# Gain of the heads on the transposed outputs, a GLA state of 128 columns, one query product, and a later first gate

## The chip, the cores and the metric

The kernel runs on one core of one Trainium2 chip. TensorE (PE) does the matrix products, with its weight loads shown apart (PEld); VectorE (DVE), ScalarE (ACT) and GpSimd (POOL) do the elementwise work; SyncE (SP) issues nearly all transfers. Each of these engines works through its own list of instructions in order. The metric is the time of one execution on the device, in microseconds, as the median of the runs.

## What is computed

A decoder layer over 2048 tokens of width 1024, in fp32, in two sub-layers, with a final norm.

```python
mod = (silu(c) @ w_ada + b_ada)                     # six rows of 1024
sh1, sc1, g1, sh2, sc2, g2 = split(mod, 6)
h = rms_norm(x) * (1 + sc1) + sh1
x = x + g1 * token_mixer(h, ...)
h = rms_norm(x) * (1 + sc2) + sh2
x = x + g2 * conv_ffn(h, ...)
return rms_norm(x) * final_gain

# in token_mixer, for 4 retention, 8 HGRN2 and 4 GLA heads of 64 values
proj = h @ w_in
o_n = attn_n @ v_n + (q_n * decay_n) @ S            # per chunk n
S   = decay * S + k_n^T @ v_n                       # GLA keys: 32 per head, others 64
o   = rms_norm(o) * silu(gate)                      # per head
return (concat(o_retention, o_hgrn2, o_gla) * head_gain) @ w_out
```

The conv_ffn has width 2816, a causal convolution of width 3 and a gated product.

## The kernel before

**Tiling.** The token mixer runs over four blocks b of 512 tokens, the conv FFN after it over two halves of 1024 tokens. Activations are kept transposed, features on the 128 partitions and tokens along the row. Every product of fp32 operands is split in a rounded high part and the rest, so it is three matmuls (`split3`, lines 246 to 248 in the function of that name): high by high, high by low, low by high. The normed input of a block is eight tiles `ha` (high and low), made from the input tiles `xn` (lines 352, 356 and 359).

**Units.** In each block the order is h0, g0, h1, h2, h3, r0, r1: four HGRN2 units of two heads, one GLA unit of four heads, two retention units of two heads. A unit projects its queries, keys, values and gates from the block's normed input, weight piece by weight piece, and hands the recurrent part to a chain of steps. After r1 follows the normed input of block b+1 and then the first half of the output projection (`out_half`); the second half (`out_finish`) comes after h0 of the next block. `out_finish` also adds the gated result to x and prepares the second norm, whose write-out for block 0 is put off until the conditioning it needs is there.

**Weight pieces.** `piece` loads 1024 columns of weight (512 KB) into one of the two `wraw` slots, ACT rounds it to the high part and DVE takes the difference as the low part. The low part is kept in memory on the first use, so later blocks fetch it. For the output projection the piece is multiplied by the heads' gain in that step, in four parts of 256 columns with a gain each (lines 236 and 239), and both parts are kept.

**Conditioning.** The 48 columns of mod are made by `ada`: a transfer of 512 KB into a `wraw` slot (line 190) and one reduction on DVE (line 197). The first 16 are made at the start. The rest wait in the list `later`, and each call of `piece` (and each quarter of the GLA value projection, `tf512`) first takes one from it. Columns 16 to 23 are the first gate (G1), which the first output projection needs; 24 to 39 are shift and scale of the second norm; 40 to 47 the second gate.

**The recurrent part.** A state S holds, for two heads, 64 columns of values each: keys on partitions, values along the row. For HGRN2 and retention S is block diagonal, 128 columns wide. For GLA the state of a pair has 64 columns; the two heads lie on different partitions. `attn_out` makes the outputs of a pair per chunk of 128 tokens. For HGRN2 and retention that is one matmul of all queries (`qn`, both heads stacked) by the state, and one of the scores by the values for each head. For GLA it is, for each head, one of the scores by the values (line 578) and one of that head's queries by the state (line 581). Queries for the scores lie in `qbd` tiles, [128, 2, 512], a plane for each head with zeros elsewhere; DVE multiplies query by decay separately for each head's rows into its plane (lines 719, 720 and 771), and ACT gathers `qn` from the planes (line 655). `transposed` turns the normed and gated outputs into `oT`, high part on ACT (line 561) and low part on DVE (line 562), for the output projection.

**Order of the work.** PE's order is that of the program. A small clock (`Clock`) adds up how long its matmuls take (`adv`), and steps of the chains are put between the projections when their due time is reached (`at`, `chain`). `rstd` makes the reciprocal root of a row norm in two steps on PE: the sum (`ssn`, line 325) and, a gap of 4.5 us by that clock later, its broadcast (`bcn`, line 335). The orders of DVE, ACT and SP are made by a scheduler from the program, with priorities given by `high_priority`.

**Constants.** `vec` has 245 columns: conditioning biases, gains, and, from column 61, the convolution's weights and biases and the final gain.

## Time and profile before

| | |
|---|---|
| median of 3 runs | 2576.79 us (2573.41 to 2576.92) |
| profiled execution | 2578.24 us |
| its span, first to last instruction | 2576.2 us |
| mean granted clock of TensorE | 0.993 |
| HBM read, written | 397.72 MB, 133.69 MB |

The stages follow from the windows of the profile: the start until about 60 us, block 0 until about 328 us, the later blocks and the last output projection until about 1300 us, then the conv FFN.

How to read it: the page's first part gives busy time of each engine, its share of the span and the count of instructions. A row of the groups or of the timeline has the line of the kernel, the engine, the operation, output and inputs by the program's names, and partitions by elements; in brackets stands how long the engine was idle before it and what ended that. The table of waits sums such idle time by who was waited for. The granted clock is that of TensorE, as a share of full speed. A timeline row of a fp32 matmul of 128 or 64 columns counts two passes ("x2") for one matmul of the program.

### The profile page before, as it was taken

How to read it: one execution, taken by the hardware profiler on the slowest of the kernel's cores; microseconds unless marked ns; L12 is line 12 of the kernel's file. 1: busy time of each engine (PE TensorE's matmuls, PEld its weight loads, DVE VectorE, ACT ScalarE, POOL GpSimd, SP SyncE). 2: the span in 40 equal slices, each digit the busy share in tenths (PEclk: the TensorE clock that was granted, in tenths of full speed). 3: DMA queues.
4: the chain of work that ended last, by engine and by line, in shares of the span. 5: the costliest groups of instructions: out<-in, count | busy, mean ns of one | idle time of the engine just before them, and what ended most of it. 6: DMA issues, size and time to landing. Idle time of an engine off the chain costs nothing.

```text
span 2576.2 us, 37281 instructions
## 1 busy us (share of the span) xinstructions
PE 2500.8 (97%) x13206; PEld 2137.1 (83%) x13206; DVE 1990.0 (77%) x3648; ACT 1116.4 (43%) x1898; POOL 168.7 (7%) x302
## 2 busy tenths in 40 slices
PE   5999999999999999999899999999989999999998
PEld 4798877998889888998788888888878888888887
DVE  8778986868778786887688888886677778778666
ACT  3433434433343234433254545555444455455442
POOL 1000010000000000000200000000001101000000
PEclk9999999999999999999999999999999999999999
DMA  8543656765687856877754444477675444447653
GB/s 302 200 155 132 214 215 227 272 217 178 212 303 271 293 176 211 316 265 258 264 186 164 163 135 163 156 256 244 220 231 169 145 154 146 145 143 245 225 191 128
DMA packets 229194, 533.89 MB, mean 207 GB/s; under 512 B 25072, under 2 KB 28176, under 8 KB 229008
## 3 DMA queue, kind: packets, MB, share of 16 engines
q1 hardware_dynamic: 224528, 516.83, 58.7%
q0 software_dynamic: 4480, 14.68, 1.6%
q8 instruction: 104, 1.70, 0.3%
q14 instruction: 82, 0.67, 0.1%
HBM read 397.72 MB, written 133.69 MB: 206 GB/s over the span
## 4 chain that ended last, share of the span: by engine, by line
PE 80%; issue 9%; DVE 6%; DMA 3%; ACT 2%; POOL 0%; SPq 0%; DVEq 0%; ACTq 0%; POOLq 0%
PE X L246 6%; PE X L248 6%; PE X L247 6%; PE lvh L622 3%; PE Z L246 3%; PE Z L248 3%; PE Z L247 3%; PE psqkvgr L248 2%; PE psqkvgr L246 2%; PE psqkvgr L247 2%; PE psvgh L246 2%; PE psvgh L247 2%; PE psvgh L248 2%; PE y L246 2%; PE y L248 2%
## 5 line engine op out<-in xcount | busy, mean ns | idle before, releaser
L246 PE MATMUL X<-B,A 128*128 128x512 f32 x572 | 223.7, 391 | 1.4 <-ACT u L1261 1.4
L247 PE MATMUL X<-B,A 128*128 128x512 f32 x572 | 222.9, 390 | 0.0
L248 PE MATMUL X<-B,A 128*128 128x512 f32 x572 | 222.8, 390 | 0.0
L988 DVE TENSOR_TENSOR dA<-rd,dA 128x512 fp32r<-128x512 f32 x154 | 106.0, 689 | 88.3 <-ACT dA L987 88.1
L987 ACT CAST dA<-rd 128x512 fp32r<-128x512 f32 x154 | 95.6, 621 | 139.8 <-PE dY L248 45.9
L988 DVE TENSOR_TENSOR A<-s,A 128x512 fp32r<-128x512 f32 x176 | 120.7, 686 | 40.5 <-ACT A L987 40.0
L987 ACT CAST A<-s 128x512 fp32r<-128x512 f32 x176 | 108.6, 617 | 72.4 <-PE Z L248 46.8
L246 PE MATMUL psvgh<-hvgh,ha 128*128 128x256 f32 x480 | 139.9, 291 | 0.0
L246 PE MATMUL dX<-dB,dA 128*128 128x512 f32 x352 | 136.9, 389 | 0.0
L247 PE MATMUL dX<-dB,dA 128*128 128x512 f32 x352 | 136.9, 389 | 0.0
L248 PE MATMUL dX<-dB,dA 128*128 128x512 f32 x352 | 136.9, 389 | 0.0
L248 PE MATMUL psvgh<-hvgh,ha 128*128 128x256 f32 x480 | 135.6, 283 | 0.0
L247 PE MATMUL psvgh<-lvgh,ha 128*128 128x256 f32 x480 | 135.6, 283 | 0.0
L246 PEld LDWEIGHTS X<-B,A 128*128 128x128 f32 x572 | 107.7, 188 | 24.4 <-ACT u L1261 2.2
L247 PEld LDWEIGHTS X<-B,A 128*128 128x128 f32 x572 | 107.7, 188 | 22.4
L248 PEld LDWEIGHTS X<-B,A 128*128 128x128 f32 x572 | 107.6, 188 | 22.4
L622 PEld LDWEIGHTS lvh<-qbh,kh 128*128 128x128 f32 x896 | 115.1, 190 | 7.8 <-issue 1.6
L246 PE MATMUL Z<-B,A 128*128 128x512 f32 x308 | 120.4, 391 | 0.0
L622 PE MATMUL lvh<-qbh,kh 128*128 128x128 f32 x896 | 120.1, 276 | 0.3 <-DVE kh L632 0.3
L247 PE MATMUL Z<-B,A 128*128 128x512 f32 x308 | 120.3, 391 | 0.0
L248 PE MATMUL Z<-B,A 128*128 128x512 f32 x308 | 120.3, 391 | 0.0
L988 DVE TENSOR_TENSOR dB<-rb,dB 128x512 fp32r<-128x512 f32 x154 | 105.4, 686 | 9.6 <-ACT dB L987 9.5
(460 smaller groups left out, 7145.9 us busy)
## 6 DMA issues: line engine op xcount, KB each, us to landing
gs<-yv SPq DMA_DIRECT2D x154, 256.0 KB, 3.0
rb<-gs SPq DMA_DIRECT2D x154, 256.0 KB, 3.9
r<-wup SPq DMA_DIRECT2D x141, 256.0 KB, 3.3
s<-sumsu SPq DMA_DIRECT2D x132, 256.0 KB, 3.0
wada<-wada SPq DMA_DIRECT2D x48, 512.0 KB, 5.0
rd<-sumsd SPq DMA_DIRECT2D x88, 256.0 KB, 3.8
rd<-wdown SPq DMA_DIRECT2D x66, 256.0 KB, 3.7
x<-xT SPq DMA_DIRECT2D x64, 256.0 KB, 5.0
```

What stands on the lines that cost most here:

```text
L246: T.matmul(ps, lhs[0], rhs[0], start=first, stop=False, skip_group_check=more)
L247: T.matmul(ps, lhs[0], rhs[1], start=False, stop=False, skip_group_check=more)
L248: T.matmul(ps, lhs[1], rhs[0], start=False, stop=last, skip_group_check=more)
L622: T.matmul(ps[:, c * P:(c + 1) * P].rearrange("p (h n s) -> p h n s", h=2, s=s), kq[:, c * P:(c + 1) * P], rhs, start=True, stop=True)
L987: S.copy(hi, src)
L988: V.tensor_tensor(lo, src, hi, op=ALU.subtract)
```

## The change

It has six parts.

1. The heads' gain is no longer multiplied into the pieces of the output weight, but into the transposed outputs, where the gain is one value for each partition: ACT's copy becomes a copy with a scale, DVE's difference a scaled difference. `both` keeps high and low part of the piece as before.
2. The GLA states have 128 columns, block diagonal like the others, and are cleared at the start. `attn_out` has one form for all: one matmul of all queries by the state, then one of scores by values for each head.
3. Query times decay is one DVE operation over all partitions, in place, and ACT copies the rows into the planes of `qbd`. The stacked queries are plane 0, after the rows of the second head have been copied into it. The tile `qn` of these units is gone.
4. Columns 16 to 23 of the conditioning are taken from `later` by the pieces from h2 on (with three places left empty), and no longer from g0 on; columns 24 to 39 after h0 of block 1, and no longer from its start. The put-off write-out of block 0 and the sums of the FFN's weights in block 1 come one unit later.
5. The gap between sum and broadcast is 8.0 us for the first norm of the next block and for the second norm of all blocks but the last.
6. `vec` has the first 117 columns; the others (`vec2`, 184 columns from column 61) are loaded after the mixer's buffers are released, before the last `out_finish`; the convolution and the final gain read it (not shown below). The mask has 320 columns instead of 448.

```diff
@@ -137,10 +137,10 @@
 
-    vec = pc.tile([P, NV], F32, tag="vec", name="vec")
-    nc.sync.dma_start(vec[:], vecs)
+    vec = pc.tile([P, 117], F32, tag="vec", name="vec")
+    nc.sync.dma_start(vec[:], vecs[:, 0:117])
     c_all = pc.tile([P, NC_], F32, tag="cst", name="c_all")
-    m_all = p1.tile([P, 448], U32, tag="msk", name="m_all")
+    m_all = p1.tile([P, 320], U32, tag="msk", name="m_all")
@@ -209,10 +209,14 @@
 
-    def piece(src, name, key, gain=None, ahead=50):
-
-        if later:
-            ada(later.pop(0))
+    def ada_next():
+        m = later.pop(0) if later else None
+        if m is not None:
+            ada(m)
+
+    def piece(src, name, key, both=False, ahead=50):
+
+        ada_next()
@@ -222,22 +226,13 @@
             nc.sync.dma_start(raw[:], src)
-            if gain is None:
-                S.copy(hi[:], raw[:])
-                if key + "l" in kept:
-                    nc.sync.dma_start(lo[:].bitcast(F32), kept[key + "l"][:])
-                else:
-                    V.tensor_tensor(lo[:], raw[:], hi[:], op=ALU.subtract)
-                    keep(key + "l", lo[:])
+            S.copy(hi[:], raw[:])
+            if key + "l" in kept:
+                nc.sync.dma_start(lo[:].bitcast(F32), kept[key + "l"][:])
             else:
-                n = 1024 // len(gain)
-                for i, g in enumerate(gain):
-                    sl = slice(i * n, (i + 1) * n)
-                    S.activation(hi[:, sl], raw[:, sl], AF.Copy, scale=g)
-                for i, g in enumerate(gain):
-                    sl = slice(i * n, (i + 1) * n)
-                    V.scalar_tensor_tensor(lo[:, sl], raw[:, sl], g, hi[:, sl], op0=ALU.mult, op1=ALU.subtract)
-                keep(key + "h", hi[:])
+                V.tensor_tensor(lo[:], raw[:], hi[:], op=ALU.subtract)
+                if both:
+                    keep(key + "h", hi[:])
@@ -289,8 +284,7 @@
             src = win[i + half:i + half + 3:2][:, :, sub * 512:(sub + 1) * 512].rearrange("a p n -> p a n")
-            if later:
-                ada(later.pop(0))
+            ada_next()
@@ -490,7 +484,7 @@
         bc1[b] = new_bc1(b)
-        clock.at(22.0, rstd(acc, f"n1_{b}", bc1[b][:], lambda: done.add(("n1", b))))
+        clock.at(22.0, rstd(acc, f"n1_{b}", bc1[b][:], lambda: done.add(("n1", b)), gap=8.0))
@@ -511,10 +505,9 @@
 
-    states = [p1.tile([P, NS, 64 if i == 4 else P], F32, tag=f"S{i}", name=f"S{i}") for i in range(7)]
-    for i, st in enumerate(states):
-        if i != 4:
-            G.memset(st[:], 0.0)
+    states = [p1.tile([P, NS, P], F32, tag=f"S{i}", name=f"S{i}") for i in range(7)]
+    for st in states:
+        G.memset(st[:], 0.0)
@@ -558,27 +551,22 @@
         oT = pa.tile([P, 2, TB], F32R, tag="a4k", name="oT" + name)
-        S.copy(oT[:, 0, :], ps[:])
-        V.tensor_tensor(oT[:, 1, :], ps[:], oT[:, 0, :], op=ALU.subtract)
+        g = vec[:, V_HG + pos:V_HG + pos + 1]
+        S.activation(oT[:, 0, :], ps[:], AF.Copy, scale=g)
+        V.scalar_tensor_tensor(oT[:, 1, :], ps[:], g, oT[:, 0, :], op0=ALU.mult, op1=ALU.subtract)
...
 
-    def attn_out(name, b, attn, v, q, Sst, qn=None):
+    def attn_out(name, b, attn, v, qn, Sst):
...
             oc = ps[:, c * P:(c + 1) * P]
-            cs = slice(c * P, (c + 1) * P)
             inter = not (b == 0 and c == 0)
-            both = inter and qn is not None
-            st = Sst[:, (b * NCH + c) % NS, :]
-            if both:
-                T.matmul(oc, qn[:, cs], st, start=True, stop=False)
+            if inter:
+                T.matmul(oc, qn[:, c * P:(c + 1) * P], Sst[:, (b * NCH + c) % NS, :], start=True, stop=False)
             for hh in range(2):
-                oo = oc[:, hh * 64:hh * 64 + 64]
-                T.matmul(oo, attn[:, (c * 2 + hh) * P:(c * 2 + hh + 1) * P], v[:, c, hh * 64:hh * 64 + 64],
-                         start=not both, stop=hh == 1 if both else not inter)
-                if inter and not both:
-                    T.matmul(oo, q[:, hh, cs], st, start=False, stop=True)
+                T.matmul(oc[:, hh * 64:hh * 64 + 64], attn[:, (c * 2 + hh) * P:(c * 2 + hh + 1) * P],
+                         v[:, c, hh * 64:hh * 64 + 64], start=not inter, stop=hh == 1 or not inter)
@@ -641,18 +629,15 @@
             yield LEVEL_GAP[two]
-        qn = None
...
             S.copy(kT[:].rearrange("p c n -> p (c n)"), ps[:])
-            if not two:
-                q, rows = subs[0][:2]
-                qn = late("qn" + name)
-                for hh, (r0, r1) in enumerate(rows):
-                        S.copy(qn[r0:r1, :], q[r0:r1, hh, :])
+            for q, rows, v, sg in subs:
+                r0, r1 = rows[1]
+                S.copy(q[r0:r1, 0, :], q[r0:r1, 1, :])
@@ -662,7 +647,7 @@
                     for hh, (r0, r1) in enumerate(rows):
-                        es = slice(0, 64) if two else slice(64 * hh, 64 * hh + 64)
+                        es = slice(64 * hh, 64 * hh + 64)
@@ -682,7 +667,7 @@
                                 dd.unsqueeze(3).to_broadcast([P, NCH, 2, 64]), op=ALU.mult)
-            ps = attn_out(f"{name}_{i}", b, at, v, q, Sst, qn)
+            ps = attn_out(f"{name}_{i}", b, at, v, q[:, 0, :], Sst)
@@ -715,8 +700,9 @@
         q = new_qbd(nm, rows)
+        V.tensor_tensor(sq[:], sq[:], f[:], op=ALU.mult)
         for hh, (r0, r1) in enumerate(rows):
-            V.tensor_tensor(q[r0:r1, hh, :], sq[r0:r1, :], f[r0:r1, :], op=ALU.mult)
+            S.copy(q[r0:r1, hh, :], sq[r0:r1, :])
@@ -762,13 +748,14 @@
         V.tensor_tensor(qk[:], qs[:], kq[:], op=ALU.mult)
+        V.tensor_tensor(qs[:], qs[:], f[:], op=ALU.mult)
...
             for hh, (r0, r1) in enumerate(rows):
-                V.tensor_tensor(q[r0:r1, hh, :], qs[r0:r1, :], f[r0:r1, :], op=ALU.mult)
+                S.copy(q[r0:r1, hh, :], qs[r0:r1, :])
@@ -857,7 +844,7 @@
         yield 3.0
-        ps = attn_out(nm, b, at, v, q, Sst, qn)
+        ps = attn_out(nm, b, at, v, qn, Sst)
@@ -901,8 +888,7 @@
         return piece(wout[half * 4 + i], f"wo{b}_{half}_{i}", f"o{half * 4 + i}",
-                     gain=[vec[:, V_HG + 4 * half + k:V_HG + 4 * half + k + 1] for k in range(4)],
-                     ahead=250 if (b, half) == (0, 0) else 600 if (b, half) == (NB - 1, 1) else 50)
+                     both=True, ahead=250 if (b, half) == (0, 0) else 600 if (b, half) == (NB - 1, 1) else 50)
@@ -955,7 +941,7 @@
             done.add(("n2", b))
-        clock.at(4.0, rstd(acc, f"n2_{b}", bc[:], then if b else lambda: put_off.append(then)))
+        clock.at(4.0, rstd(acc, f"n2_{b}", bc[:], then if b else lambda: put_off.append(then), gap=8.0 if b < NB - 1 else 4.5))
@@ -1046,15 +1032,13 @@
         W0 = startup()
-    nc.sync.dma_start(m_all[:], msk)
+    nc.sync.dma_start(m_all[:], msk[:, 0:320])
...
         pos = 0
-        if b == 1:
-            later += range(24, 40)
@@ -1062,9 +1046,11 @@
             pos += 2 if kind == "g" else 1
-            if b == 0 and i == 0:
-                later += range(16, 24)
-            if b == 1 and i == 2:
+            if b == 0 and i == 2:
+                later += [16, 17, 18, 19, 20, None, 21, None, 22, None, 23]
+            if b == 1 and i == 0:
+                later += range(24, 40)
+            if b == 1 and i == 3:
@@ -1073,8 +1059,8 @@
                 early_sums(i - 1)
-            if b and i >= (3 if b == 1 else 1):
-                for _ in range(2 if b == 2 else 1):
+            if b and i >= (4 if b == 1 else 1):
+                for _ in range(2 if b == 2 or (b, i) == (1, 6) else 1):
@@ -1450,6 +1436,8 @@
     halo = pg.tile([P, 2 * NF + 4, 2], F32, tag="halo", name="halo")
+    vec2 = pg.tile([P, NV - V_CW], F32, tag="vec2", name="vec2")
+    nc.sync.dma_start(vec2[:], vecs[:, V_CW:NV])
...
     for i in (7, 4):

```

The order on **PE** in the GLA unit of block 1, where the outputs of its first pair are made. S_111 is the GLA state, qbg the queries, atg the scores, vg the values. Before, the last of the sixteen rows and what follows them:

```order
L578 MATMUL og_0_4615<-vg_0_3935,atg_0_4040 128x64
L581 MATMUL og_0_4615<-S_111,qbg_0_3928 128x64
L246 MATMUL psvgh_2_0_4599<-hvgh_2_0_4601,ha_2_2762 128x256
L247 MATMUL psvgh_2_0_4599<-lvgh_2_0_4602,ha_2_2762 128x256
L248 MATMUL psvgh_2_0_4599<-hvgh_2_0_4601,ha_2_2762 128x256
```

And now, the last of four such pairs of rows:

```order
L566 MATMUL og_0_4525<-S_111,qbg_0_3862 128x128
L568 MATMUL og_0_4525<-vg_0_3869,atg_0_3974 128x64 x2
L241 MATMUL psvgh_2_0_4509<-hvgh_2_0_4511,ha_2_2758 128x256
L242 MATMUL psvgh_2_0_4509<-lvgh_2_0_4512,ha_2_2758 128x256
L243 MATMUL psvgh_2_0_4509<-hvgh_2_0_4511,ha_2_2758 128x256
```

Of sixteen matmuls for a pair twelve are left: the eight by the state became four, each over both heads.

The order on **DVE** at the end of block 0. xn_7 and ha_7 are the last tile of block 1's normed input, S_113 the state of the last retention pair, or and orsr the outputs of r0 and their norm, wada a conditioning column. Before:

```order
L843 SCALAR_TENSOR_TENSOR S_113<-S_113,c_all,ur_1_3180 64x64
L158 SCALAR_TENSOR_TENSOR orsr_0_3143<-nw,orsr_0_3143 128x8
L352 SCALAR_TENSOR_TENSOR xn_7_2789<-xn_7_2789,mod,bc_1_1855 128x512
L156 SCALAR_TENSOR_TENSOR nw<-orsr_0_3143 128x8
L562 TENSOR_TENSOR oTh_3_0_3162<-oTh_3_0_3157,oTh_3_0_3162 128x512
L157 TENSOR_TENSOR nw<-nw,omsr_0_3140 128x8
L197 ISA wada_3214,mod<-wada_3214,c_act,vec 128x1024
L197 ISA mod 128x1
L158 SCALAR_TENSOR_TENSOR orsr_0_3143<-nw,orsr_0_3143 128x8
L359 SCALAR_TENSOR_TENSOR ha_7_2792<-xn_7_2789,mod,ha_7_2792 128x512
```

And now:

```order
L346 SCALAR_TENSOR_TENSOR xn_6_2779<-xn_6_2779,mod,bc_1_1842 128x512
L346 SCALAR_TENSOR_TENSOR xn_7_2785<-xn_7_2785,mod,bc_1_1842 128x512
L851 TENSOR_TENSOR or_0_3103<-or_0_3091,c_all 128x512
L353 SCALAR_TENSOR_TENSOR ha_6_2782<-xn_6_2779,mod,ha_6_2782 128x512
L353 SCALAR_TENSOR_TENSOR ha_7_2788<-xn_7_2785,mod,ha_7_2788 128x512
L541 TENSOR_REDUCE omsr_0_3107<-osqr_0_3105 128x8
L828 COPY S_113<-ur_1_3147 64x64
```

Both rows of the last tile stood behind the updates of S_113 and one of them behind a column; now both stand ahead of the updates, next to those of the tile before. On **SP** the transfer of that tile stood behind one of a column; before:

```order
L499 DMA xn_6_2783<-xT 128x512
L784 DMA roper_0_5245<-rope 128x256
L190 DMA wada_3319<-wada 128x1024
L499 DMA xn_7_2789<-xT 128x512
L228 DMA lvgh_0_0_3323<-kepti2l 128x1024
```

And now:

```order
L493 DMA xn_6_2779<-xT 128x512
L231 DMA lhqh_0_3182<-kepti0l 128x1024
L493 DMA xn_7_2785<-xT 128x512
L228 DMA rvgh_0_1_3340<-win 128x1024
L231 DMA lvgh_0_0_3285<-kepti2l 128x1024
L190 DMA wada_3432<-wada 128x1024
```

The columns now come after the tile, and a kept low part of a weight piece (lhqh) stands ahead of it instead.

The order on **DVE** in the first GLA unit of block 0, at its last value pieces (lvgg are their low parts, qbh and kh the level products of h0's scores). Before:

```order
L305 TENSOR_TENSOR lvgg_2_979<-rvgg_2_976,hvgg_2_978 128x1024
L630 TENSOR_TENSOR qbh_0_687<-qbh_0_687,eh_0_675 128x16x32
L632 TENSOR_TENSOR kh_0_673<-kh_0_673,eh_0_675 128x8x32
L595 TENSOR_TENSOR eg_709<-eg_709 128x8
L197 ISA wada_973,mod<-wada_973,c_act,vec 128x1024
L197 ISA mod 128x1
L595 TENSOR_TENSOR eg_709<-eg_709 128x4
L630 TENSOR_TENSOR qbh_0_687<-qbh_0_687,eh_0_675 128x8x64
L632 TENSOR_TENSOR kh_0_673<-kh_0_673,eh_0_675 128x4x64
L197 ISA wada_1016,mod<-wada_1016,c_act,vec 128x1024
L197 ISA mod 128x1
L305 TENSOR_TENSOR lvgg_3_1022<-rvgg_3_1019,hvgg_3_1021 128x1024
```

And now:

```order
L299 TENSOR_TENSOR lvgg_3_1007<-rvgg_3_1004,hvgg_3_1006 128x1024
L618 TENSOR_TENSOR qbh_0_688<-qbh_0_688,eh_0_676 128x32x16
L620 TENSOR_TENSOR kh_0_674<-kh_0_674,eh_0_676 128x16x16
L629 COPY_PREDICATED ath_0_0_764<-m_all,lvh_0_16_932 128x32x16
L618 TENSOR_TENSOR qbh_0_688<-qbh_0_688,eh_0_676 128x16x32
L620 TENSOR_TENSOR kh_0_674<-kh_0_674,eh_0_676 128x8x32
L233 TENSOR_TENSOR lhfh_1_1085<-rhfh_1_1086,hhfh_1_1084 128x1024
```

The columns are gone from between the pieces, and the last piece's low part and that of h1 (lhfh) stand earlier against the level products.

8 lines of the change are left out of this document (4 added, 4 removed).

## The prediction

> **What bounds the kernel now.** I read the busy shares first, then the table of waits of TensorE (PE), then windows and the timeline around each wait.
>
> ```profile
> PE 2500.8 (97%) x13206; PEld 2137.1 (83%) x13206; DVE 1990.0 (77%) x3648; ACT 1116.4 (43%) x1898; POOL 168.7 (7%) x302
> ```
>
> PE is busy for 97% of a span of 2576.2 us and idle for 75.4 us. The other engines have room on average, so an instruction taken from them is worth nothing by itself. Time goes in two ways only: fewer or shorter instructions on PE, or fewer waits of PE. The second is a short list (all waits of PE of over 1 us that the change touches, with two that it does not):
>
> ```profile
> PE ssn L325 <- DVE san L346: 6.6, 1, 6.6
> ...
> PE oTh L559 <- DVE oh L553: 2.7, 2, 2.4
> PE pshfh L246 <- ACT ha L356: 2.6, 1, 2.6
> ...
> PE psvgg L246 <- ACT hvgg L299: 1.6, 1, 1.6
> PE pshfh L247 <- DVE ha L359: 1.6, 1, 1.6
> PE bcn L335 <- DVE rsn L158: 1.4, 2, 1.1
> PE alg L743 <- ACT snh L707: 1.4, 1, 1.4
> PE psvgg L247 <- DVE lvgg L305: 1.4, 2, 0.8
> ...
> PE pshfh L248 <- DVE lhfh L230: 1.3, 1, 1.3
> ...
> PE lvg L622 <- DVE qbg L771: 1.1, 2, 0.7
> ```
>
> The columns are total us, number of waits and the longest. Most of them lie in block 0, while conditioning columns (wada) are still being fetched. The whole change lies in the token mixer, the first 1300 us.
>
> **The change, part by part.** I take the sum against the profiled execution (2578.24 us, 1.45 us over the median of 2576.79) and carry the difference to the median.
>
> *GLA state of 128 columns.* Two rows that follow each other give the pace of PE in this place:
>
> ```profile
> 1099.30 0.39 PE L581 MATMUL og<-S,qbg 128*128 128x64 f32 x2
> 1099.52 0.39 PE L578 MATMUL og<-vg,atg 128*128 128x64 f32 x2
> ```
>
> One matmul of the program is two passes on the chip, and the next begins 0.22 us later (16 of them in a row keep a step of 0.223). The trace has 120 passes of line 581, so 60 matmuls, two for each of 30 chunk-and-pair cases (the first chunk has no state). The change makes one of each two, over 128 columns. What a pass over 128 columns costs is shown by the state update of the same unit:
>
> ```profile
> 169.66 1.95 PE L661 MATMUL ug<-vg,kTg 128*128 128x128 f32 x16
> 171.36 0.36 PE L246 MATMUL psvgh<-hvgh,ha 128*128 128x256 f32 x1
> ```
>
> Sixteen passes of 128 columns take 1.70 us, 0.106 us each; a pass of 64 columns took 0.112. Width is free here, so 30 matmuls go: 30 x 0.223 = **-6.7 us**, all on PE, hidden by nothing. The bounds are 0 (a wide pass costs two narrow ones) and -6.7; I take -6.7, since the wide row is of the same form.
>
> [...]
>
> *Conditioning columns moved (`later`).* Each is a 512 KB DMA into one of the two `wraw` slots that the weight pieces use too, and one reduction on DVE:
>
> ```profile
> 100.28 1.28 DVE L197 CUSTOM_DVE_ANT_0 wada<-wada,c_act,vec 128x1024 f32<-128x1024 f32 x1 [0.22 <-DMA wada<-wada]
> 101.56 1.04 ACT L299 CAST hvgg<-rvgg 128x1024 fp32r<-128x1024 f32 x1 [0.55 <-DMA rvgg<-win]
> 102.64 1.22 DVE L305 TENSOR_TENSOR lvgg<-rvgg,hvgg 128x1024 fp32r<-128x1024 f32 x1 [1.06 <-ACT hvgg L299]
> wada<-wada SPq DMA_DIRECT2D x48, 512.0 KB, 5.0
> ```
>
> A piece comes after a column in the same slots, its cast waits for the DMA, its low half on DVE waits for the cast, and PE for both. In the first GLA unit and the HGRN2 unit after it these waits of PE are 1.6 + 1.4 + 1.3 us. In the new order no column stands there at all (the first comes some 30 DVE rows after the last of these pieces): **-4.3 us** (bounds 0 and -4.3). The cast of a GLA piece also stood between `sfh` and `snh` on ACT, for which the low-rank product waited 1.4 us; it now comes earlier, by about the cast's 1.0 us: **-1.0** (0 to -1.4).
>
> With fewer rows on DVE ahead of it, the output of the first HGRN2 pair comes earlier as well:
>
> ```profile
> 130.95 0.66 PE L559 MATMUL oTh<-c_all,oh 128*128 128x128 f32 x4 [2.44 <-DVE oh L553]
> ```
>
> DVE was full in the 20 us before it, and a reduction (1.28 us) at 113 us and the four narrow query products are no longer ahead: **-2.0** (0 to -2.4).
>
> The eight columns do not vanish. They land on the units h2, h3 and r0. What is there to take them is this (columns: start and end, length, busy time of PE, PEld, DVE, ACT, POOL, granted clock, DMA share, GB/s):
>
> ```profile
> 60.00:140.00 80.00, 73.08 (x408) 59.97 (x409) 66.20 (x131) 31.01 (x56) 1.99 (x3) 1.00 0.56 198
> 140.00:330.00 190.00, 185.50 (x1194) 167.03 (x1193) 157.61 (x374) 71.72 (x149) 9.08 (x16) 0.99 0.47 164
> ```
>
> From 140 to 330 us DVE has 32 us free and the DMA share is 0.47. Eight columns add 8 x 1.36 = 10.9 us of DVE; the stage loses two later columns (2.7), HGRN2 query products and the narrow gain products. A unit there is longer per piece than the GLA unit, so slots come round more slowly. I charge half of what the same eight cost where they stood: **+2.0** (0 to +4.3, were all of it to come back).
>
> *The passage from block 0 to block 1.* This is the largest loss outside the start. PE waits 2.6 us for the last tile of the next block's normed input and 1.6 us for its low half, and then (columns: busy PE, granted clock, DMA share, GB/s):
>
> ```profile
> 324.00:326.00 2.00, 0.00 (x0) 1.00 0.00 0
> 326.00:328.00 2.00, 0.49 (x1) 0.83 0.00 0
> 328.00:330.00 2.00, 1.89 (x5) 0.50 0.68 258
> ...
> 332.00:334.00 2.00, 2.00 (x6) 0.50 0.99 391
> ```
>
> The clock is granted at 0.50 for the 6 us after it, which costs another 3.0 us. So the event is 4.2 + 3.0 = 7.2 us. Why the tile is late:
>
> ```profile
> 311.22 0.33 SPq L190 DMA_DIRECT2D wada<-wada  x1
> 312.42 0.33 SPq L499 DMA_DIRECT2D xn<-xT  x1
> ```
> ```profile
> 319.10 1.41 DVE L359 SCALAR_TENSOR_TENSOR ha<-xn,mod,ha 128x512 fp32r<-128x512 f32 x2
> ...
> 324.49 0.74 DVE L352 SCALAR_TENSOR_TENSOR xn<-xn,mod,bc 128x512 f32<-128x512 f32 x1
> ...
> 326.02 1.28 DVE L197 CUSTOM_DVE_ANT_0 wada<-wada,c_act,vec 128x1024 f32<-128x1024 f32 x1
> ...
> 327.31 0.75 DVE L359 SCALAR_TENSOR_TENSOR ha<-xn,mod,ha 128x512 fp32r<-128x512 f32 x1
> ```
>
> On SP the last input tile stands behind a column that waits for its slot; on DVE its scaling stands behind the state updates of the last retention pair, and its low half behind a column. In the new order nothing of that is ahead: on DVE both rows come before the state updates, on SP the column comes after the tile. Both rows stand with those of the tiles before it, which ran at 319.1, so the low half would be done at about 322, before the idle stretch. **-7.2** (0 to -7.2). Next in line for PE is the piece of the query product, and that was cast long before:
>
> ```profile
> 310.16 1.03 ACT L226 CAST hhqh<-rhqh 128x1024 fp32r<-128x1024 f32 x1
> ```
>
> *Longer gaps for the row norm.* PE stood 1.4 us before the broadcast of the reciprocal root; with 8.0 instead of 4.5 us of other work between the two products that goes: **-1.4** (0 to -1.4).
>
> *One query operation and the gain on the outputs.* These take work from DVE and give some to ACT.
>
> ```profile
> L719 DVE TENSOR_TENSOR qbh<-sqh,fh 64x512 f32<-64x512 f32 x32 | 21.8, 683 | 0.3
> L771 DVE TENSOR_TENSOR qbg<-qg,fg x16: 673/682/689, 88.2 to 1031.2; 32x512 f32<-32x512 f32 x16
> L655 ACT COPY qnh<-qbh 64x512 f32<-64x512 f32 x32 | 19.8, 618 | 5.4 <-DVE qbh L630 4.5 <-DVE nw L156 0.6
> L239 DVE SCALAR_TENSOR_TENSOR lwo<-rwo,vec,hwo 128x256 fp32r<-128x256 f32 x32 | 14.3, 479 | 0.6 <-ACT hwo L236 0.6
> ```
>
> A DVE row of 64 or 32 partitions costs 0.68 us, the same as a full one, so DVE loses 16 x 0.683 (HGRN2) and 12 x 0.682 (GLA) = 19.1 us. ACT gains 48 copies and loses a net 8 (32 of `qn` become 24): 40 x 0.618 = 24.7 us on an engine that is busy 43%. The gain: DVE exchanges 4 x 0.479 for one pass of 1.22 us (as `lvgg` above), eight times, some -5.6 us, and pays 32 x 0.05 us for the scaled form (0.74 of line 352 against 0.69 of a plain 128x512). All of this lies beside PE; its price is 0. Only one wait of PE hangs on the query itself, the 1.1 us of block 1. There the last of four DVE products is replaced by one product and four copies on ACT behind a weight cast: between -1.1 and, if the cast (1.04 us) and copies are late in each of four blocks, +4; I take **-0.5**.
>
> *Left as it was.* The wait of 6.6 us for the last block's sum of squares stays. DVE stands there for a transfer in a stretch in which the DMA engines are full, and the new order has the same row ahead of the sum:
>
> ```profile
> 1285.43 0.69 DVE L1187 TENSOR_TENSOR s<-rv,s 128x512 f32<-128x512 f32 x1 [7.97 <-DMA sumsu<-s]
> ```
>
> The second load of constants adds 94 KB to it, far under 1 us: 0.
>
> Sum: -6.7 - 4.3 - 1.0 - 2.0 + 2.0 - 7.2 - 1.4 - 0.5 = **-21.1 us**, so 2557.1 for the profiled execution and 2555.7 beside the median: **2556**.
>
> **The rivals.**
> 1. *The waits only move.* DVE's order is made anew in the whole mixer, and for each wait that goes another appears. Then the matmuls alone count, less the +2.0: 2576.8 - 4.7 = 2572. For it: late in block 0 DVE is nearly full, as the row below shows. Against: from 140 to 330 us PE was idle for 4.5 us, and 4.2 of them are the passage, so there is cover.
>
> ```profile
> 280.00:300.00 20.00, 20.00 (x108) 17.09 (x107) 19.37 (x42) 10.22 (x25) 1.04 (x2) 1.00 0.79 277
> ```
>
> 2. *The passage stays.* Its tile depends on a transfer and on three engines; if one of them is late, 7.2 us remain: 2563.
> 3. *A wide pass costs two narrow ones.* The first term is 0: 2562. [...]
> 4. *Slower: the moved columns starve h2 to r0.* Both `wraw` slots are held until DVE has read a column, so the piece behind it comes late, and each stop long enough to lower the clock costs what the passage did, 7.2 us. It decides from the fourth such stop: -23.1 + 4 x 7.2 = +5.7, so 2582. For it: eleven pieces carry eight columns there. Against it: the same crowd cost 4.3 us where it stood, with no loss of clock.
> 5. *The last wait goes too.* If the full DMA stretch at 1276 us clears sooner, 6.6 us and some of the half clock behind it go: 2546.
>
> **How the numbers follow.** Forecast 0.50; the waits only move 0.13; the passage stays 0.20; the wide pass 0.05; slower 0.07; the last wait too 0.05. A measurement of this kernel tells about 0.2% (5.2 us) from no change, so faster means under 2571.6: 0.50 + 0.20 + 0.05 + 0.05 = 0.80; same 0.13; slower 0.07. The range goes from the fifth case to the edge of the first: 2546 to 2572. It covers the bounds of the single terms except where several fail at once. The likeliest case by itself is 2551 to 2561.
>
> **What would show it.** In the new trace: 60 passes of the wide form where 120 narrow ones were, in the same 0.22 us a pair; no wait for `hvgg`, `lvgg` or `lhfh` at 90 to 115 us; PE busy through the start of block 1 at a clock of 1.00; no wait on the norm's broadcast there; the 6.6 us still there. Waits of PE for weight pieces between 190 and 300 us, or for `qbg` copies on ACT, would make the prediction wrong.

## The result, and the profile after

The median is 2559.31 us (2559.0 to 2562.22, 5 runs) against 2576.92 us (2573.41 to 2578.67, 5 runs) of the kernel before on the same chip: a ratio of 0.9936, with an interval of 0.9923 to 0.995. That is 17.6 us less by the medians, where 21.1 were forecast, and 2559.3 lies in the stretch that was called the likeliest, 2551 to 2561. The profiled executions have spans of 2576.2 and 2557.2 us, 19.0 apart.

The busy times on the page of the changed kernel:

```profile
PE 2493.1 (97%) x13146; PEld 2132.7 (83%) x13146; DVE 1973.8 (77%) x3596; ACT 1139.0 (45%) x1914; POOL 169.6 (7%) x303
```

PE is busy 7.7 us less, with 60 passes fewer, and its idle time falls from 75.4 to 64.1 us, by 11.3. Both halves of the 19.0 are thus visible: work and waits. The table of waits of PE in the changed kernel (total us, number, longest):

```profile
...
PE ssn L319 <- DVE san L340: 6.0, 1, 6.0
PE pshfh L241 <- ACT sgg L532: 4.1, 1, 4.1
...
PE oTh L552 <- DVE oh L546: 1.6, 4, 0.7
...
PE psvgh L242 <- DVE lvgh L233: 1.1, 1, 1.1
...
PE alg L729 <- ACT snh L692: 0.5, 1, 0.5
```

The waits for `ha` at the passage (2.6 + 1.6), for `hvgg`, `lvgg` and `lhfh` in block 0 (1.6 + 1.4 + 1.3) and for the first norm's broadcast on `rsn` (1.4) are gone. The wait for the last sum of squares is still there, 6.0 for 6.6. One wait has grown: 4.1 us for `sgg`, the gates of the GLA unit. The kernel before has it with 3.1, in another block:

```profile
PE pshfh L246 <- ACT sgg L539: 3.1, 1, 3.1
```

One wait is new, the 1.1 us for `lvgh`, the low part of a weight piece, at 201.61 us. Windows of the changed kernel at three places of the prediction (length, busy PE, PEld, DVE, ACT, POOL, granted clock, DMA share, GB/s):

```profile
60.00:140.00 80.00, 79.24 (x476) 67.97 (x474) 59.07 (x123) 33.59 (x60) 2.00 (x3) 1.00 0.48 167
140.00:330.00 190.00, 188.70 (x1203) 169.79 (x1203) 166.02 (x383) 75.11 (x146) 12.28 (x21) 1.00 0.54 188
```
```profile
314.00:316.00 2.00, 2.00 (x10) 1.65 (x10) 1.81 (x9) 0.72 (x2) 0.00 (x0) 1.00 0.00 0
316.00:318.00 2.00, 2.00 (x12) 1.74 (x10) 1.94 (x5) 1.69 (x3) 0.00 (x0) 1.00 0.59 168
```

PE fills 79.24 of the 80 us from 60 to 140 (73.08 before). The matmul for which the old kernel stood still until 326.04 us starts at 314.96 in the new one, without a wait and at full clock.

The best single reading is the **lead**: the start of the same matmul in both timelines, the difference in us (negative: the changed kernel is earlier). What happens between two rows of this table is what that stretch gained.

| the same matmul, time before | place | lead | step |
|---|---|---|---|
| 60.2 | `alg`, first GLA unit | -1.1 | -1.1 |
| 150.4 | h2 starts | -8.2 | -7.1 |
| 186.7 | h3 starts; first GLA outputs are behind it | -9.5 | -1.3 |
| 282.0 | output projection of block 0 | -8.3 | +1.2 |
| 357.3 | behind the passage to block 1 | -17.0 | -8.7 |
| 408.0 | GLA unit of block 1 | -17.6 | -0.6 |
| 511.7 | h3 of block 1 | -20.4 | -2.8 |
| 712.8 | GLA unit of block 2 | -18.5 | +1.9 |
| 751.5 | first pieces of h1, block 2 | -22.6 | -4.1 |
| 1020.9 | GLA unit of block 3 | -23.2 | -0.6 |
| 1054.6 | first pieces of h1, block 3 | -16.0 | **+7.2** |
| 1207.8 | last output projection | -17.1 | -1.1 |
| 2576.2 | end | -19.0 | -1.9 |

Up to 511 us the lead grows where the terms of the prediction lie. What it did not have are two steps of the same kind: 4.1 us gained in block 2 and 7.2 lost in block 3, both at the first matmul of h1 behind the GLA unit. The timelines of PE, ACT and DVE in the changed kernel at the loss (start, duration, row; in brackets the wait and what ended it):

```profile
1028.73 0.77 PE L241 MATMUL pshfh<-ha,hhfh 128*128 128x512 f32 x1 [4.05 <-ACT sgg L532]
```
```profile
1028.22 0.27 ACT L531 COPY vg<-psvgg 128x128 f32<-128x128 f32 x1 [2.13 <-DVE sgg L533]
```
```profile
1022.06 0.62 DVE L533 TENSOR_TENSOR sgg<-sgg,psvgg 128x128 f32<-128x128 f32 x2 [1.05 <-ACT sgg L532]
1022.90 0.69 DVE L974 TENSOR_TENSOR eo<-es,eo 128x512 fp32r<-128x512 f32 x1 [0.22 <-ACT eo L973]
1023.51 1.29 DVE L618 TENSOR_TENSOR qbg<-qbg,eg 128x512 f32<-128x512 f32 x2
...
1025.05 2.43 DVE L629 COPY_PREDICATED atg<-m_all,lvg 128x512 f32<-128x512 uint32 x2
1027.27 0.72 DVE L668 TENSOR_TENSOR og<-vg,dotg 128x512 f32<-128x512 f32 x1
1027.91 0.86 DVE L533 TENSOR_TENSOR sgg<-sgg,psvgg 128x128 f32<-128x128 f32 x4
```

`psvgg` holds values and gates of four chunks, in four banks; each bank has both pairs of heads. The kernel empties the banks for the first pair (ACT copies `vg`, ACT takes the sigmoid, DVE multiplies it in), then for the second. DVE did two products of the first pair at 1022.06, a low part `eo` of the FFN was ready next, and then the intra-chunk work of the GLA unit (`qbg`, `atg`) until 1027.9. The copy of the second pair on ACT waited 2.13 us for the product that DVE had not yet made, and PE waited 4.05 us for the banks. PE's own windows there (length, busy PE, granted clock, DMA share, GB/s):

```profile
1026.00:1028.00 2.00, 0.00 (x0) 0.87 0.97 320
1028.00:1030.00 2.00, 1.27 (x3) 0.50 0.99 336
1030.00:1032.00 2.00, 2.00 (x6) 0.50 0.51 209
1032.00:1034.00 2.00, 2.00 (x7) 0.50 0.94 377
1034.00:1036.00 2.00, 2.00 (x15) 0.93 0.84 279
```

The wait is 4.05 us, the half clock behind it makes 7.2 of it. The kernel before has the same event in block 2. Its DVE there:

```profile
736.35 0.48 DVE L540 TENSOR_TENSOR sgg<-sgg,psvgg 128x128 f32<-128x128 f32 x2
736.75 0.69 DVE L895 TENSOR_TENSOR wsu<-wsu,wsu 128x512 f32<-128x512 f32 x1
737.35 1.29 DVE L630 TENSOR_TENSOR qbg<-qbg,eg 128x512 f32<-128x512 f32 x2
...
741.75 0.87 DVE L540 TENSOR_TENSOR sgg<-sgg,psvgg 128x128 f32<-128x128 f32 x4
```

A weight sum `wsu` stands where `eo` stands in the new kernel. PE waited 3.10 us at 742.57. So the change removed the event in one block and made it in another.

### The profile page after: what moved, and what is told of

The parts are those of the page before. It is cut to its first block, busy times and chain, and to the rows that moved or that the text cites. A ratio compares the mean times of both kernels' runs of the same rounds, so it can differ in the third digit from the quotient of the medians.

```text
span 2557.2 us, 37116 instructions
## 1 busy us (share of the span) xinstructions
PE 2493.1 (97%) x13146; PEld 2132.7 (83%) x13146; DVE 1973.8 (77%) x3596; ACT 1139.0 (45%) x1914; POOL 169.6 (7%) x303
## 4 chain that ended last, share of the span: by engine, by line
PE 78%; issue 9%; DVE 5%; DMA 4%; ACT 1%; SPq 0%; POOL 0%; DVEq 0%; ACTq 0%; POOLq 0%
PE X L241 6%; PE X L242 6%; PE X L243 6%; PE Z L241 3%; PE Z L242 3%; PE Z L243 3%; PE lvh L610 3%; PE y L241 2%; PE y L243 2%; PE y L242 2%; PE psqkvgr L243 2%; PE psqkvgr L241 2%; PE psqkvgr L242 2%; PE psvgh L242 2%; PE psvgh L241 2%
```

## The experiments

Each ran beside the kernel before on the same chip. Differences between kernels of several chips go by their ratios, times 2577 us; the interval of one ratio is about 3.5 us to either side, so a difference of two of them is known to some 5 us. Where less is claimed the lead in the trace carries it. But a trace is one execution, and after like waits the clock falls in one and not in another (last section), which moves a lead by some 1.5 to 1.7 us.

**1. The gate's banks emptied bank by bank (`fix`).** The changed kernel, with the order in the GLA unit turned: for each bank ACT takes both pairs, and only then DVE multiplies.

```diff
-        for i in range(2):
-            tok_evac4(subs[i][2:], pss, 256 * i)
+        for c, ps in enumerate(pss):
+            for i, (q, rows, v, sg) in enumerate(subs):
+                S.copy(v[:, c, :], ps[:, 256 * i:256 * i + P])
+                S.activation(sg[:, c, :], ps[:, 256 * i + P:256 * i + 256], AF.Sigmoid)
+            for i, (q, rows, v, sg) in enumerate(subs):
+                V.tensor_tensor(sg[:, c, :], sg[:, c, :], ps[:, 256 * i + P:256 * i + 256], op=ALU.mult)
```

> The changed kernel with one edit: in the GLA unit, copies and sigmoids of both pairs are taken from a bank of values and gates before the two products on DVE, so the bank is given back early. Theory A (the 4.1 us wait for the second pair's gates in block 3 and the half clock behind it are a new loss, made by DVE's order, and ate part of the gain): the wait goes and the time falls by 4.1 + 3 = 7 us, to about 2552. Rival B (the wait is set by TensorE's own pace or by ACT's added query copies ahead of the gates): ACT's load is the same, so the wait stays or moves to the next product, and the time stays within 2 us of 2559.

2554.56 us (2551.73 to 2555.92), ratio 0.9911 [0.9897, 0.9924], so 6.4 us less than the changed kernel by the ratios, 4.8 by the medians. The wait for `sgg` is gone in every block, and the matmul that had waited 4.05 us now runs on:

```profile
1025.67 0.39 PE L241 MATMUL pshfh<-ha,hhfh 128*128 128x512 f32 x1
```

The lead over the kernel before is 23.2 us at the last output projection, where the changed kernel had 17.1: 6.1 gained. Some of it is given back behind the mixer (the FFN's wait for the final norm's sum of squares, `n3a`, is 3.8 us here and 1.4 there). The mechanism is shown: at this place the order in which the banks are emptied made the wait. Since this event comes and goes with DVE's order, the parts of the change were undone on this base.

**2. The same edit on the kernel before (`before_fix`).**

> The kernel before with the one edit of run fix (copies and sigmoids of both GLA pairs ahead of the two products, for each bank). Theory A (before the change the same event stood in block 2, a wait of 3.1 us with half clock behind it, and the change moved it to block 3): that wait goes, 4 to 5 us faster than before, with no wait for the gates in any block. Rival B (in block 2 the wait was for a sum of FFN weights on DVE, another cause): a wait of 2 to 3 us stays at the start of the next HGRN2 unit, within 2 us of before.

2573.91 us (2569.99 to 2578.2, 10 runs), ratio 0.9985 [0.9972, 0.9998], 3.9 us less. Between 712 and 751 us the lead goes from +4.3 to -0.7, so 5.0 us come back with the wait; the profiled execution had lost 4.7 earlier, between 90 and 150 us, where it has the waits of the kernel before nearly unchanged (`psvgg` for `hvgg` 1.8 for 1.6), so these waits do not explain it; its mean granted clock is 0.991, that of the kernel before 0.993. The event is a property of the code before, worth 4 to 5 us in block 2.

**3. GLA states of 64 columns again (`fix_narrow`).** On `fix`, part 2 undone:

```diff
...
+                    T.matmul(oo, attn[:, (c * 2 + hh) * P:(c * 2 + hh + 1) * P], v[:, c, hh * 64:hh * 64 + 64],
+                             start=True, stop=False)
+                    T.matmul(oo, q[:, hh, c * P:(c + 1) * P], Sst[:, (b * NCH + c) % NS, :], start=False, stop=True)
...
-                es = slice(64 * hh, 64 * hh + 64)
+                es = slice(0, 64) if two else slice(64 * hh, 64 * hh + 64)
```

> The kernel of run fix with the GLA states of 64 columns and their four matmuls per chunk again, all else as there. Theory A (width is free in this stream, 30 matmuls of two passes less): 6.7 us slower than fix. Rival B (a pass over 128 columns costs two of 64): the same time as fix, within 1.5 us.

2562.03 us (2556.75 to 2566.03), 0.994 [0.9926, 0.9954]: 7.5 us more than `fix`. In the trace the four GLA output steps lose 1.3, 1.8, 1.6 and 1.8 us of lead against `fix`, 6.6 in all (block 0 gets 1.4 of them back before its end, where it no longer waits for `lvgh`). In the changed kernel the same four steps gain 1.3, 1.8, 1.1 and 1.8 against the kernel before; a new wait of 0.5 us for a state takes from the third. The group of wide passes in the changed kernel (ns least, median, most; first and last start):

```profile
L566 PE MATMUL og<-S,qbg x60: 272/276/348, 166.5 to 1084.4; 128*128 128x128 f32 x60
```

60 wide passes took the place of 120 narrow ones, and a wide pass lasts 276 ns at the median, one of 64 columns 275 (in `fix_narrow`). Had a wide pass cost two narrow ones, as rival 3 has it, this undo would have been worth nothing; the run does not agree.

**4. Columns 16 to 23 early again (`fix_g1_early`).** On `fix`, the first half of part 4 undone:

```diff
-            if b == 0 and i == 2:
-                later += [16, 17, 18, 19, 20, None, 21, None, 22, None, 23]
+            if b == 0 and i == 0:
+                later += range(16, 24)
```

> The kernel of run fix with columns 16 to 23 of the conditioning taken by the pieces from g0 on again, all else as there. Theory A (the columns between the pieces made the waits for the GLA value pieces and the first HGRN2 output in block 0, and cost less where they stand now): waits of TensorE for these pieces of about 4 us come back between 90 and 115 us, 2.4 us before the first transposed output, 1 us before the low-rank product; the time rises by 5 to 7 us. Rival B (they cost as much wherever they stand): the same time within 2 us, since the waits in h2 to r0 go instead.

2560.18 us (2554.23 to 2564.23), 0.9934 [0.992, 0.9948]: 5.9 us more than `fix`. The waits of block 0 come back, though between 90 and 115 us only 1.9 of the 4 that were expected. From its table of waits, and the PE timeline:

```profile
PE alg L729 <- ACT snh L692: 1.4, 1, 1.4
...
PE pshfh L243 <- DVE lhfh L233: 1.2, 1, 1.2
```
```profile
127.64 0.85 PE L552 MATMUL oTh<-c_all,oh 128*128 128x128 f32 x4 [2.38 <-DVE oh L546]
```

At 150 us its lead is 1.7 where `fix` has 8.1, so 6.4 are lost, some 1.6 of them by the lowered clock behind the wait of 2.38 (0.80 and 0.86 from 125 to 135 us, last section); at 282 us 3.6 against 8.2, so 1.8 of them return. Those 1.8 us are what the eight columns cost where the change puts them.

**5. Columns 24 to 39 early again (`fix_cols24`).** On `fix`, the second half of part 4 undone:

```diff
+        if b == 1:
+            later += range(24, 40)
...
-            if b == 1 and i == 0:
-                later += range(24, 40)
```

> The kernel of run fix with columns 24 to 39 of the conditioning taken from the start of block 1 again, gain as changed. Its order keeps both rows of block 1's last input tile ahead of the state updates, though two columns stand ahead of the tile's transfer on SP. Theory A (DVE's order decides at the passage): no wait there, within 2 us of fix. Rival B (the columns on SP and in the slots decide): 4.2 us of waits there and 6 us slower than fix.

2565.94 us (2564.36 to 2568.13), 0.9949 [0.9937, 0.9962]: 9.8 us more than `fix`, the dearest single undo. But the wait at the passage is not the one of the kernel before. A row each of DVE, SP, ACT and PE there:

```profile
317.39 1.28 DVE L197 CUSTOM_DVE_ANT_0 wada<-wada,c_act,vec 128x1024 f32<-128x1024 f32 x1
```
```profile
318.71 0.33 SPq L228 DMA_DIRECT2D rhqh<-win  x1
```
```profile
323.38 1.04 ACT L229 CAST hhqh<-rhqh 128x1024 fp32r<-128x1024 f32 x1 [5.11 <-DMA rhqh<-win]
```
```profile
324.47 0.79 PE L241 MATMUL pshqh<-ha,hhqh 128*128 128x512 f32 x1 [7.39 <-ACT hhqh L229]
```

The tile `ha` is in time here, and the query piece is late instead: its transfer is issued at 318.71, when the reduction that ends at 318.7 has read the column in its `wraw` slot, and that reduction stood behind the state updates. So to have the tile early in DVE's order is not enough, and theory A has fallen; that the columns in the two slots decide the passage stands. Which of the tile or the piece is late is then a matter of order. This piece is the one that the prediction took for safe, as its cast was long done in the kernel before.

**6. The gain on the weights and columns 24 to 39 early (`fix_gain_cols`).** Parts 1 and the second half of 4 undone together (edits 5 and 7).

> The kernel of run fix with two parts undone: the gain multiplied into the weight pieces again, and columns 24 to 39 taken from the start of block 1 again. In its order the last input tile of block 1 stands behind a column on SP and behind the state updates of the last retention pair on DVE, as before the change. Theory A (that order made the wait at the passage from block 0 to block 1): TensorE waits there again, 4.2 us and 3 us of half clock, 7 to 9 us slower than fix. Rival B (the passage was cured because TensorE comes to it earlier or later against the transfers, whatever the order): no such wait, under 2 us slower.

2560.76 us (2558.11 to 2565.09), 0.9937 [0.9924, 0.995]: 6.7 us more than `fix`. Its table of waits has the passage of the kernel before to a tenth, and one more:

```profile
...
PE pshfh L250 <- DVE sgg L775: 3.9, 1, 3.9
...
PE pshfh L250 <- ACT ha L359: 2.6, 1, 2.6
...
PE pshfh L251 <- DVE ha L362: 1.6, 1, 1.6
```

With the old gain the tile is late, with the new one the query piece (experiment 5); with the columns moved neither. The row for `sgg`, in block 1, shows that experiment 1 makes its wait rarer, not impossible. It costs 6.5 us of lead here, so the 6.7 us are not the price of the passage alone.

**7. The gain on the weights (`fix_gain`).** On `fix`, part 1 undone:

```diff
-            S.copy(hi[:], raw[:])
...
+                for i, g in enumerate(gain):
+                    sl = slice(i * n, (i + 1) * n)
+                    S.activation(hi[:, sl], raw[:, sl], AF.Copy, scale=g)
...
-        S.activation(oT[:, 0, :], ps[:], AF.Copy, scale=g)
+        S.copy(oT[:, 0, :], ps[:])
```

> The kernel of run fix with the gain multiplied into the weight pieces again, columns as changed. Its order keeps both rows of block 1's last input tile ahead of the state updates. Theory A (the passage needs both parts undone to come back; the gain itself lies beside TensorE and costs nothing): the same time as fix, within 2 us, no wait at the passage. Rival B (the gain's place alone made the wait at the passage): 4.2 us of waits there and 6 us slower.

2552.97 us (2550.23 to 2556.44), 0.9898 [0.9885, 0.9912]: 3.3 us **less** than `fix`, and no wait at the passage (the lead grows by 8.6 us there, 8.7 in the changed kernel). In block 0 the lead at 282 us is 10.6 instead of 8.2, in the main since the wait of 1.1 for `lvgh` is missing; 4.8 us are lost again at 506, half of them in a 2.43 us wait for `kTh`. At 1300 us the two leads are 23.2 and 23.1. So the first part of the change brought nothing, and may have cost some 3 us: the runs say so within their noise, the profiled executions do not.

**8. Query products on DVE again (`fix_query`).** On `fix`, part 3 undone:

```diff
-        V.tensor_tensor(sq[:], sq[:], f[:], op=ALU.mult)
         for hh, (r0, r1) in enumerate(rows):
-            S.copy(q[r0:r1, hh, :], sq[r0:r1, :])
+            V.tensor_tensor(q[r0:r1, hh, :], sq[r0:r1, :], f[r0:r1, :], op=ALU.mult)
...
```

The GLA unit is edited in the same way.

> The kernel of run fix with query times decay made on DVE for each head again, and no copies on ACT. Theory A (19 us of DVE and 25 us of ACT lie beside TensorE): the same time as fix, within 1.5 us. Rival B (DVE's relief carries part of the gain in block 0, where it was full): 3 us slower or more, with waits of TensorE for DVE between 60 and 330 us. Rival C (ACT's copies delay the queries): 1 to 2 us faster, since the wait for the query copy at the first GLA value product goes.

2558.28 us (2556.66 to 2559.84), 0.9918 [0.9905, 0.9932]: 1.8 us more than `fix`. At 282 us the lead is 5.3 instead of 8.2, and the PE timeline shows the place:

```profile
188.09 1.13 PE L610 MATMUL lvh<-qbh,kh 128*128 128x128 f32 x8 [0.53 <-DVE kh L620]
203.02 0.39 PE L242 MATMUL psvgh<-lvgh,ha 128*128 128x256 f32 x1 [2.04 <-DVE lvgh L233]
```

`fix` waits 1.1 for the same `lvgh`, and not for this `kh`: 1.4 us of the loss are longer waits for DVE. The rest, some 1.6, is the clock, which is granted at 0.56 and 0.59 from 204 to 208 us here and at 1.00 in `fix`. The relief of DVE was not worth nothing: it carries the moved columns in h2, by 1.4 us or more. The 1.8 us of the runs alone would not tell Theory A from Rival B.

**9. The short gap again (`fix_gap`).** On `fix`, part 5 undone:

```diff
-        clock.at(22.0, rstd(acc, f"n1_{b}", bc1[b][:], lambda: done.add(("n1", b)), gap=8.0))
+        clock.at(22.0, rstd(acc, f"n1_{b}", bc1[b][:], lambda: done.add(("n1", b))))
...
-        clock.at(4.0, rstd(acc, f"n2_{b}", bc[:], then if b else lambda: put_off.append(then), gap=8.0 if b < NB - 1 else 4.5))
+        clock.at(4.0, rstd(acc, f"n2_{b}", bc[:], then if b else lambda: put_off.append(then)))
```

> The kernel of run fix with the gap between sum and broadcast of the row norms at 4.5 us everywhere again. Theory A (the gap took away the waits for the reciprocal root): they come back, 1.4 us in all, and the time rises by 1 to 2 us. Rival B (they went because DVE has less to do): no such wait, the same time within 1 us.

2559.19 us (2556.36 to 2560.4), 0.992 [0.9907, 0.9934]: 2.3 us more than `fix`, 4.1 by the lead at the last output projection. Its waits for the broadcast, and the longest (`fix` has one, of 1.4 us, at the last broadcast, whose gap part 5 leaves as it was):

```profile
PE bcn L329 <- DVE rsn L158: 4.7, 4, 2.2
```
```profile
382.38 1.13 PE L329 MATMUL bcn<-c_all,rsn 128*128 128x128 f32 x8 [2.16 <-DVE rsn L158]
```

The clock is granted at 0.50 from 384 to 386 us, and the lead falls by 3.8 us between 386 and 401.

**10. Part 4 alone on the kernel before (`before_cols`).** The lines of the change's diff on `ada_next` and `later`, and nothing else of it.

> The kernel before with one part of the change alone: columns 16 to 23 taken from h2 on, columns 24 to 39 after h0 of block 1, the put-off write-out and the sums of the FFN's weights one unit later with them. Theory A (the columns in the two weight slots made the waits in block 0 and at the passage): the waits for the GLA value pieces, the first HGRN2 output and the passage go, the new waits in h2 to r0 cost about 2 us; 12 to 15 us faster than before, at 2562 to 2565 where before is 2577. Rival B (the passage needs the gain out of the weight pieces as well): only the waits in block 0 go, 5 to 7 us faster, at about 2571.

2569.71 us (2566.33 to 2573.41), 0.9965 [0.9952, 0.9979]: 9.0 us less than the kernel before, where 12 or more were expected. Its lead is 8.2 us at 150 and grows by 8.6 at the passage, as in the whole change, so the mechanism is right. What is missing is lost in between: 4.4 us from 150 to 282, nearly all of it by waits of 0.52 and 2.04 us and the half clock behind them (0.67 and 0.50 from 204 to 208), around

```profile
204.60 0.52 PE L251 MATMUL psvgh<-lvgh,ha 128*128 128x256 f32 x1 [2.04 <-DVE lvgh L234]
```

and 3 us at the second norm's broadcast (a wait of 2.78 for `rsn`). Without the other parts, of which the query's relief and the longer gap bear on these two places, the moved columns cost more than 2 us.

**11 and 12. The last weight sum in place (`fix_inplace`, `fix_gain_inplace`).** Both let the last of the first four weight sums of the FFN be written over its own operand, so that it needs no buffer of its own; the second has the gain on the weights as well.

```diff
-        V.tensor_tensor(s4[:], rv[1], s2[:], op=ALU.subtract)
+        s4 = rv[1] if first else s4[:]
+        V.tensor_tensor(s4, rv[1], s2[:], op=ALU.subtract)
...
```

> The kernel of run fix with the last of the first four sums of FFN weights written over its own operand, so DVE needs no free slot for it ahead of the last block's sums of squares. Theory A (the wait that the change left, at the end of the mixer, is DVE standing for a slot whose transfer crawls in a full stretch of DMA): the wait of 4.5 to 6.0 us for the sum of squares falls under 2 us, the half clock behind it goes, 5 to 8 us faster than fix. Rival B (the transfers of the output weight and the residual pace this stretch): DVE's wait goes and TensorE's stays within 2 us of what it was; the time as fix, within 2 us.

> The kernel of run fix_gain (gain multiplied into the weight pieces) with the same write in place. Theory A as for fix_inplace: 5 to 8 us faster than fix_gain. If the gain's place is neutral as run fix_gain showed within its interval, it ends within 3 us of fix_inplace; if the gain on the outputs costs the 2.5 us that TensorE lost to it in block 0 of run fix, it ends 2 to 4 us under fix_inplace.

`fix_inplace` has 2554.02 us (2551.3 to 2554.97), 0.9902 [0.9889, 0.9916], 2.3 us less than `fix`; the wait for the last sum of squares shrinks from 4.45 to 1.92 us, but the wait for `Y` a little later grows from 2.9 to 6.0. `fix_gain_inplace` has 2550.3 us (2548.71 to 2552.17), 0.989 [0.9876, 0.9903], the fastest of all: 11.9 us less than the changed kernel, and 2.1 less than `fix_gain`. Both miss the 5 to 8 us of Theory A. In the second the wait is back:

```profile
1263.39 1.84 PE L328 MATMUL ssn<-c_all,san 128*128 128x1 f32 x8 [5.55 <-DVE san L349]
```

So the buffer is not what sets this wait by itself. The gain on the weights is worth 3.1 us here, 3.3 in experiment 7: twice the same sign, though the intervals touch each time. By the lead at 1300 us it is 1.9 here and nothing there.

## Why the prediction came out as it did

- **GLA state, -6.7: right.** 6.6 us at the four output steps, 7.5 by the medians. Rival 3 is out. In the changed kernel itself the steps are 6.1.
- **Columns out of block 0's GLA pieces, low-rank product, first output, -7.3 together: right.** The lead was 8.2 at 150 us. At `alg` the wait fell from 1.4 to 0.5 us, as forecast (1.0). The undo loses 6.4, some 1.6 of them by the clock.
- **The moved columns, +2.0: right in size** (1.2 in the trace, 1.8 by the undo), **but for a reason that the sum had at nothing.** The step "its price is 0" for query and gain failed: it took DVE's 19 us of relief as lying beside PE. Without it the same columns cost some 3 us more (`fix_query`; about half of it is waits, the rest the lowered clock), or 4.4 in place of 1.2 (`before_cols`, which lacks the other parts too). One of the prediction's own signs against itself appeared here, a wait for a weight piece between 190 and 300 us: the 1.1 us for `lvgh`. It was small enough to stay within the term.
- **The gain on the outputs, 0: not settled.** Two comparisons have 3.3 and 3.1 us against it, each within its noise, and their profiled executions nothing and 1.9. What the trace shows of it is the `lvgh` wait in block 0.
- **The passage, -7.2: right.** Of the 8.7 gained, 7.7 are the wait and the half clock (4.2 us of waits, and 0.50 granted from 328 to 334 us in the kernel before); 1.0 comes behind them, where a wait of 0.84 us for `or` (at 353.76 in the kernel before) is gone too. The cause was told too narrowly: not the tile's place on SP and DVE by itself, but the columns in the slots, which make either the tile or the query piece late.
- **The longer gap, -1.4: right as to the wait,** which is gone (1.15 us at 397 and 0.29 at 215). In the changed kernel only 0.6 of it shows between 357 and 408 us, where two waits of 0.4 for a state stand instead. By the undo it is worth more, 2.3, as the wait is 2.16 there and the clock behind it is granted at 0.50 from 384 to 386 us.
- **The query in block 1, -0.5: the wait went, the reason is open.** The two waits for `qbg` (0.41 and 0.74 us at 424 to 426 in the kernel before) are gone, and the lead grows by 1.5 us between 408 and 430. But it grows by as much in `fix_query`, where the products are back on DVE, and in `before_cols`, so the single product is not needed for it.
- **The last wait, left as it was: right,** 6.0 for 6.6. DVE still stands for the same transfer:

```profile
1267.89 0.69 DVE L1173 TENSOR_TENSOR s<-rv,s 128x512 f32<-128x512 f32 x1 [7.29 <-DMA sumsu<-s]
```

- **What had no term:** the emptying of the gate's banks, 4.1 gained in block 2 and 7.2 lost in block 3. Together +3.1, near the difference between forecast and result (3.5 by the medians, 2.1 by the spans). That the two agree is in part luck: at 511 us the lead was 20.4 where the terms due by then make 17.5 (21.1 without the 16 of 30 wide-state cases of blocks 2 and 3, 3.6), and 1.9 of it were gone again at 713, ahead of either bank. This is rival 1 on a small scale: DVE's order is made anew, and a wait moved. The prediction listed the waits "that the change touches" and left the 3.1 us for `sgg` out, since no edit concerns it; an order made by a scheduler is touched everywhere.

The undone parts make 7.5 + 5.9 + 9.8 + 2.3 + 1.8 - 3.3 = 24.0 us. They lead from `fix` back to `before_fix`, and these two are 19.1 us apart by their ratios. The sum is thus 5 us too large: each undo carries its noise, and the parts lean on each other, as the query's relief and the moved columns do. Of the 24.0 the column moves carry two thirds, the wide state a third. Part 6, and the later place of the put-off write-out and of the weight sums in part 4, were not undone by themselves.

Two things stay open: whether the gain on the outputs costs anything, and what sets the wait at the end of the mixer. The DMA engines are at a share of 0.97 to 0.99 from 1240 to 1270 us in the changed kernel, which fits a transfer that comes late, but no run thinned that traffic out.

## What to carry to other kernels

Move transfers that nobody needs soon away from a seam between stages, above all when they pass through the slots that the next stage's weights use: the two moves, 15.7 us by their undos, were worth more than the wide state, 7.5. When a scheduler makes the order, list every wait of 3 us or more as able to come or go, also those that no edit touches, and test parts of a change on a base in which such a wait has been removed. Where two engines read the same buffer in turn, let the first take all that it needs before the second starts.

## What the hardware showed

- One wait is dearer than its length when the clock falls behind it: 4.05 us made 7.2 of lead in block 3, with 0.50 granted from 1028 to 1034 us; 3.10 us made 4 to 5 in block 2 of the kernel before, with 0.50 from 744 to 746. By the windows the share of the clock lost from 1026 to 1036 us in the changed kernel is 3.4 us, as much as 6.8 us at half, and from 742 to 748 us in the kernel before 1.7 us, as much as 3.4 at half (length, busy PE, granted clock, DMA share, GB/s):

```profile
742.00:744.00 2.00, 1.44 (x6) 0.94 0.86 301
744.00:746.00 2.00, 2.00 (x7) 0.50 0.64 256
746.00:748.00 2.00, 2.00 (x9) 0.71 0.94 303
```

- The length of a wait does not settle whether the clock falls behind it, and it fell behind single waits well under 3 us: 2.38 us in `fix_g1_early`, 2.16 in `fix_gap` (experiment 9), 1.12 in `fix_cols24`. The 2.38 us wait at 127.64 in `fix_g1_early` has a granted clock of 0.80 and 0.86 in the ten microseconds from 125 to 135; the 2.44 us wait at 130.95 in the kernel before, for the same operand, kept 1.00, and so did the 2.78 us wait for `rsn` at 387.33 in `before_cols`. PE's windows in the first, then in the second (length, busy PE, PEld, DVE, ACT, POOL, granted clock, DMA share, GB/s):

```profile
125.00:130.00 5.00, 2.62 (x11) 1.98 (x10) 4.68 (x9) 1.74 (x2) 0.00 (x0) 0.80 0.32 128
130.00:135.00 5.00, 5.00 (x34) 4.69 (x33) 3.75 (x7) 1.46 (x2) 0.00 (x0) 0.86 0.63 210
```
```profile
130.00:135.00 5.00, 4.05 (x28) 3.76 (x29) 4.87 (x10) 1.32 (x2) 0.00 (x0) 1.00 0.14 55
```

Even the wait of 1.12 us for `lvgh` splits in this way: in `fix_cols24` the clock falls behind it, in `fix`, where it is as long and at the same place, it does not (length, busy PE, granted clock, DMA share, GB/s; the row and the first windows are of `fix_cols24`, the last of `fix`). It costs `fix_cols24` about 1.5 us of lead.

```profile
201.41 0.49 PE L242 MATMUL psvgh<-lvgh,ha 128*128 128x256 f32 x1 [1.12 <-DVE lvgh L233]
```
```profile
200.00:202.00 2.00, 0.88 (x6) 0.88 0.00 0
202.00:204.00 2.00, 2.00 (x11) 0.50 0.92 283
```
```profile
200.00:202.00 2.00, 0.88 (x7) 1.00 0.00 0
202.00:204.00 2.00, 2.00 (x20) 1.00 0.80 262
```

Why the clock falls behind one wait and not behind a like one is not shown by these runs.
